# Joining the q and k products of two attentions into one token-major product of 512 columns

## Chip, cores and metric

One core of a Trainium2 chip runs the whole kernel. The metric is device time in microseconds (us). The kernel before takes 2263.23 us, the median of three runs (2261.22 to 2263.38).

## What is computed

One block of a hybrid model, for 512 tokens of width 2048: a normalization, one wide input projection, four mixers side by side, a gate and an output projection with the residual. Each mixer has 1024 columns. Cut to what matters here:

```python
h = rms_norm(x, norm_g)
p = h @ w_in                                  # 2048 -> all inputs of the mixers and the gate z
p_rwkv, p_fox, p_gdn, p_diff, z = split(p)
y = concatenate([
    rwkv7_time_mix(p_rwkv, ...),              # recurrence over tokens, 16 heads of 64
    forgetting_attention(p_fox, ...),         # q, k normalized per head of 64; softmax with forget bias
    gated_deltanet(p_gdn, ...),               # chunked delta rule, 8 heads of 128
    differential_attention(p_diff, ...),      # q, k normalized per head of 64; two softmax maps, subtracted
])
x = x + (y * silu(z)) @ w_out
```

Both attentions normalize q and k over heads of 64 columns before the scores.

## The kernel before

**Products.** All large products run on TensorE in a split form: an operand is cast to a short format (`hh`, `wh`), the remainder is kept beside it (`hl`, `wl`), and three matrix multiplies (hh·wh, hl·wh, hh·wl) stand for one. The normalized input lies in `hh` and `hl`, 16 tiles of 128 rows by 512 tokens. Weights come in tiles of 1024 columns by 128 partitions: SP issues the load into `wr` (three buffers), ScalarE casts it into `wh` (line 313, two buffers), VectorE subtracts to get `wl` (line 314, two buffers).

**Two forms of product.** `gemm_fm` is feature-major: 128 weight columns are the stationary operand, 512 tokens move, one accumulator bank, 48 multiplies. `gemm_tm` is token-major: 128 tokens are stationary, 256 weight columns move (128 each of two column blocks, `ca` and `cb`), 192 multiplies of 256 columns for all 512 tokens, in two accumulator banks of two token tiles each. It runs over four weight parts; with `late` (used for `fqk` alone) the order is part 0 and part 1 of the first bank, then both parts of the second. There are two banks of the kind `acc`; the products take them in turn.

**The loop.** `main()` is one stream over eight groups `j`. A group's products are, in order: r, k, v of the recurrence; v, k, q of the delta rule (`gv`, `gk`, `gq`); `fqk` (q and k of the forgetting attention); `vv` (the values of both attentions; for group 0 made ahead, and two gate products stand in its place); `dqk` (q and k of the differential attention). Everything else (recurrence chain, delta chain, triangular inverses, the attentions) is written as generators, the threads, that issue a few small instructions and yield the time until they want to go on.

**The planner.** The order of TensorE's instructions is written out by the program: a clock `pe[0]` adds up modelled TensorE time, and a thread whose time has come puts its instructions between two steps of the stream. A yielded time is stretched by `SLACK = 1.25`. The stream may also yield a condition, such as `("gdn_chain", j - 1)` after the `gk` product; until it holds, threads alone go on. PSUM banks have planned times: `bank(tag, name, hold)` takes one, `release(name, wait)` says when it comes free, `free(tag)` waits for it. The delta chain holds its bank `cg` for one chunk of 128 tokens, four chunks in a row. The other engines' orders are found by a scheduler, by the bands of priority that `band()` sets: chains first, then weight loads and splits, read-outs of products, the rest. Each engine, and each queue for loads and stores, serves its instructions in that order.

**q and k of an attention.** `qk_evac` reads each bank out on ScalarE (a square and two copies) and sums the squares on VectorE; `qk_heads` makes the inverse roots (`rsqrt`, three Newton steps on VectorE), scales, transposes on TensorE and splits q and k. `fox` uses the first pair of `qa` tiles, `diff` waits for `fox` and uses the next. The masks `ones`, `tri` and `sgt` lie in the pool of constants `cp`.

Of the kernel before, what the change touches and what calls it, by code (L numbers as in the profile page):

```python
# [10 lines left out]
F32 = mybir.dt.float32  # L11
# [3 lines left out]
AF = mybir.ActivationFunctionType  # L15
# [39 lines left out]
def hybrid_kernel(ctx: ExitStack, tc: tile.TileContext, ins, out, steps=tuple(range(NJ)), ydbg=None, tail=True):  # L55
# [124 lines left out]
    def mm_tm(accs, t, part, wh, wl, ks=range(4), paired=False):  # L180
        o = accs[t // 2][:, (t % 2) * 256:(t % 2) * 256 + 256]
        ts_ = slice(t * P, (t + 1) * P)
        if paired:
            for k4 in ks:
                k = part * 4 + k4
                sl = slice(k4 * 256, (k4 + 1) * 256)
                MM(o, hh[:, k, ts_], wh[:, sl], start=(k == 0 and t % 2 == 0), stop=False)
                MM(o, hh[:, k, ts_], wl[:, sl], start=False, stop=False)
                MM(o, hl[:, k, ts_], wh[:, sl], start=False, stop=(k == KT - 1 and t % 2 == 1))
            return  # L190
# [36 lines left out]
    for t in range(NT):  # L227
# [23 lines left out]
        for part in range(4):  # L251
            wr, wh, wl = w0[part]
            if t == 0:
# [7 lines left out]
    ones = cp.tile([P, P], F32, name="ones")  # L261
    nc.gpsimd.memset(ones, 1.0)
    tri = cp.tile([P, P], F32, name="tri")
    nc.gpsimd.affine_select(out=tri, in_=ones, pattern=[[1, P]], compare_op=ALU.is_ge,
                            fill=0.0, base=0, channel_multiplier=-1)
    sgt = cp.tile([P, P], F32, name="sgt")
    nc.gpsimd.affine_select(out=sgt, in_=ones, pattern=[[-1, P]], compare_op=ALU.is_gt,
                            fill=0.0, base=0, channel_multiplier=1)
# [5 lines left out]
    mask2 = cp.tile([P, P], F32, name="mask2")  # L274
    for half in range(2):
        rows = slice(half * C, (half + 1) * C)
        nc.gpsimd.affine_select(out=mask2[rows, 0:C], in_=ones[rows, 0:C], pattern=[[1, C]],
                                compare_op=ALU.is_gt, fill=0.0, base=0, channel_multiplier=-1)
        nc.gpsimd.affine_select(out=mask2[rows, C:], in_=ones[rows, 0:C], pattern=[[1, C]],
                                compare_op=ALU.is_ge, fill=0.0, base=0, channel_multiplier=-1)  # L280
# [61 lines left out]
    def gemm_tm(ca, cb, name, evac, need, late=False):  # L342

        accs, ws = None, {}
        order = [(part, b) for part in range(4) for b in range(2)]
        if late:
            order[0:4] = [(0, 0), (1, 0), (0, 1), (1, 1)]
        for part, b in order:
            if part not in ws:
                band(PRIO_W)  # L350
                wr = wtile()
                load_tm(wr, part, ca, cb)
                ws[part] = wsplit(wr)
            for t in (2 * b, 2 * b + 1):
                for k4 in (0, 2):
                    band(PRIO_GEMM)
                    if accs is None:
                        accs = [pacc(f"acc_{name}_{i}") for i in range(2)]
                    mm_tm(accs, t, part, *ws[part], (k4, k4 + 1), name.startswith("fqk"))
                    yield  # L360
            if part == 3:
                yield need
                band(PRIO_EVAC)
                evac(b, accs[b])

# [103 lines left out]
    def gates(fab0):  # L469
        fold = mp.tile([C, 32], F32, name="fold", tag="at", bufs=4)  # L470
# [412 lines left out]
    def gdn_chain(j, st, XG):  # L883
# [3 lines left out]
        for c in range(NT):  # L887
# [21 lines left out]
            MM(ps[:, 3 * P:4 * P], GA[:, c, 1, :], Y, start=True, stop=True)  # L909
            if c < NT - 1:  # L910
                band(PRIO_CHAIN)
# [4 lines left out]
                band(PRIO_MIX)  # L916
            if c:
                ACT(ot[:, c, :], ps[:, P:2 * P], AF.Copy, scale=eg[:, 0, c, j:j + 1])
# [3 lines left out]
            release(f"pG{j}_{c}", 5.0)  # L922
# [138 lines left out]
    def qk_evac(j, kind):  # L1061
        tiles = []

        def evac(b, acc):
            if b == 0:
                tiles.extend(mp.tile([P, NT, P], F32, name=f"{s}a{kind}{j}", tag="qa", bufs=2) for s in "qk")
                tiles.append(mp.tile([P, 16], F32, name=f"ss{kind}{j}", tag="ss", bufs=2))
            qa, ka, ss = tiles
            av = acc.rearrange("p (t s f) -> p t s f", t=2, s=2)
            sq = mp.tile([P, T], F32, name=f"sq{kind}{j}_{b}", tag="tmp", bufs=2)  # L1070
            ACT(sq, acc, AF.Square)
            for s, dst in enumerate((qa, ka)):
                nc.scalar.copy(dst[:, 2 * b:2 * b + 2, :], av[:, :, s])
            nc.vector.tensor_reduce(ss[:, 8 * b:8 * b + 8], sq.rearrange("p (g f) -> p g f", f=C),
                                    axis=AX.X, op=ALU.add)

        return tiles, evac

    def qk_heads(j, ev, kind):
        qa, ka, ss = ev  # L1080
        gi = 0 if kind == "fox" else 2
        TS(ss, ss, 1.0 / C, 1e-6, op0=ALU.mult, op1=ALU.add)
        rs = rsqrt(mp, ss, 16, "qk", f"{kind}{j}")
        yield 3.0
        rv = rs.rearrange("p (t s h) -> p t s h", t=NT, s=2)
        for s, dst in enumerate((qa, ka)):
            dv = dst.rearrange("p t (h f) -> p t h f", f=C)
            TT(dv, dv, rv[:, :, s].unsqueeze(3).to_broadcast([P, NT, 2, C]), op=ALU.mult)
# [3 lines left out]
        for s, src in enumerate((qa, ka)):  # L1092
# [94 lines left out]
    def diff(j, ev, V):  # L1187
        yield from until("fox", j)
# [93 lines left out]
    def main():  # L1282
# [15 lines left out]
        for j in steps:  # L1298
# [37 lines left out]
            spawn(2.0, fox(j, fev, values, nb))  # L1336
# [154 lines left out]
```

## Time and profile before

| what | value |
|---|---|
| median of three runs | 2263.23 us |
| the profiled execution's own time | 2262.35 us |
| its span, first to last instruction | 2260.5 us |
| TensorE busy (PE) | 2221.2 us, 98% |
| weight loads into TensorE (PEld) | 1906.3 us, 84% |
| VectorE (DVE) | 1370.0 us, 61% |
| ScalarE (ACT) | 795.5 us, 35% |
| GpSimd (POOL) | 228.3 us, 10% |
| mean granted TensorE clock | 0.994 of full speed |
| moved by DMA | 225.81 MB, mean 100 GB/s |

A busy TensorE is not one at its peak: matrix multiplies overlap, so the distance between two starts tells more than the length of one. In the timeline a row gives start, duration, engine, line, operation, out<-in, shapes and count; a bracket at the end is the idle time before it and what ended it. The group around 1083 us, used below, is group 5 of the loop.

### The profile page before, as it was taken

The numbers are of one execution on the slowest core, as the hardware profiler recorded it, in microseconds if no ns is written. First come the engines' busy times: TensorE is split into PE (matmuls) and PEld (weight loads), VectorE is DVE, ScalarE is ACT, GpSimd is POOL, SyncE is SP. The second block draws the span as 40 slices with busy tenths as digits, with TensorE's granted clock in tenths as the row PEclk, the third lists the DMA queues.
The fourth block names the chain that finished last, engine by engine and source line by source line (L and its number), as shares of the span: only waits on it lengthen the run. The fifth ranks groups of instructions, "written<-read, shape, count | busy, mean of one in ns | idle before, by whom it ended". The sixth has DMA issues, their size and how long they took to land.

```text
span 2260.5 us, 37244 instructions
## 1 busy us (share of the span) xinstructions
PE 2221.2 (98%) x14604; PEld 1906.3 (84%) x14604; DVE 1370.0 (61%) x3601; ACT 795.5 (35%) x1456; POOL 228.3 (10%) x474
## 2 busy tenths in 40 slices
PE   7999999999999999999999999999999999999999
PEld 6789789879978977987997897798888888888887
DVE  6368487677856858767785785876553334322222
ACT  4233443343343344334334334433332233321121
POOL 2200121102102112110210201211000000100000
PEclk9999999999999999999999999999999999999999
DMA  5433323323322332332332233233346444655443
GB/s 167 104 87 95 96 70 94 96 61 89 97 72 72 89 97 70 94 97 63 87 102 65 74 87 96 67 99 101 99 139 178 120 123 121 164 135 117 113 124 75
DMA packets 320850, 225.81 MB, mean 100 GB/s; under 512 B 16911, under 2 KB 284370, under 8 KB 320162
## 3 DMA queue, kind: packets, MB, share of 16 engines
q1 hardware_dynamic: 298722, 187.05, 31.3%
q0 software_dynamic: 8128, 14.84, 3.0%
q10 hardware_dynamic: 13824, 21.54, 2.9%
q8 instruction: 115, 1.88, 0.4%
q14 instruction: 61, 0.50, 0.1%
HBM read 203.40 MB, written 19.97 MB: 99 GB/s over the span
## 4 chain that ended last, share of the span: by engine, by line
PE 95%; DVE 2%; DMA 1%; ACT 1%; issue 1%; POOL 1%; ACTq 0%; SPq 0%; DVEq 0%; POOLq 0%
PE acc_z L70 16%; PE acc_o L70 15%; PE acc_fqk L70 8%; PE acc_dqk L70 8%; PE acc_vv L70 8%; PE acc_v L70 4%; PE acc_k L70 4%; PE acc_r L70 4%; PE acc_gk L70 4%; PE acc_gv L70 4%; PE acc_gq L70 3%; PE pC L70 3%; PE pm L70 1%; PE pG L70 1%; PE pSf L70 1%; PE po L70 1%
## 5 line engine op out<-in xcount | busy, mean ns | idle before, releaser
L314 DVE TENSOR_TENSOR wl<-wr,wh 128x1024 fp32r<-128x1024 f32 x318 | 388.7, 1223 | 535.8 <-ACT wh L313 529.8
L313 ACT CAST wh<-wr 128x1024 fp32r<-128x1024 f32 x318 | 333.8, 1050 | 770.3 <-PE acc_o L70 232.1
L70 PE MATMUL acc_z<-hh,wh 128*128 128x512 f32 x512 | 204.5, 399 | 0.0
L70 PE MATMUL acc_z<-hh,wl 128*128 128x512 f32 x512 | 199.8, 390 | 0.0
L70 PE MATMUL acc_z<-hl,wh 128*128 128x512 f32 x512 | 199.6, 390 | 0.0
L70 PE MATMUL acc_o<-wh,gl 128*128 128x512 f32 x512 | 183.6, 389 | 0.0
L70 PE MATMUL acc_o<-wl,gh 128*128 128x512 f32 x512 | 177.4, 389 | 0.0
L70 PE MATMUL acc_o<-wh,gh 128*128 128x512 f32 x512 | 176.2, 389 | 0.1
L70 PE MATMUL acc_fqk<-wh,hh 128*128 128x256 f32 x512 | 151.1, 295 | 0.0
L70 PE MATMUL acc_fqk<-wl,hh 128*128 128x256 f32 x512 | 145.2, 284 | 0.0
L70 PE MATMUL acc_fqk<-wh,hl 128*128 128x256 f32 x512 | 145.1, 283 | 0.0
L70 PE MATMUL acc_dqk<-wh,hh 128*128 128x256 f32 x512 | 138.3, 292 | 0.0
L70 PE MATMUL acc_dqk<-wh,hl 128*128 128x256 f32 x512 | 133.6, 283 | 0.0
L970 DVE TENSOR_TENSOR bP<-bX,bA 112x2 f32<-112x2 f32 (+30 forms) x248 | 122.0, 492 | 5.6 <-POOL bA L958 1.1
L70 PE MATMUL acc_vv<-wh,hh 128*128 128x256 f32 x448 | 120.7, 291 | 0.0
L70 PE MATMUL acc_vv<-wh,hl 128*128 128x256 f32 x448 | 116.9, 282 | 0.0
L70 PEld LDWEIGHTS acc_z<-hh,wl 128*128 128x128 f32 x512 | 96.1, 188 | 20.7
L70 PEld LDWEIGHTS acc_o<-wh,gh 128*128 128x128 f32 x512 | 96.0, 188 | 20.4 <-ACT wh L313 0.5
L70 PEld LDWEIGHTS acc_z<-hh,wh 128*128 128x128 f32 x512 | 96.2, 188 | 19.9 <-issue 0.7
L70 PEld LDWEIGHTS acc_o<-wl,gh 128*128 128x128 f32 x512 | 96.1, 188 | 20.0
L70 PEld LDWEIGHTS acc_o<-wh,gl 128*128 128x128 f32 x512 | 96.1, 188 | 20.0
L70 PEld LDWEIGHTS acc_z<-hl,wh 128*128 128x128 f32 x512 | 96.3, 188 | 18.3
(514 smaller groups left out, 5210.6 us busy)
## 6 DMA issues: line engine op xcount, KB each, us to landing
wr<-in_w_in SPq DMA_DIRECT2D x162, 512.0 KB
wr<-in_w_in SPq DMA_DIRECT2D x184, 256.0 KB
wr<-in_w_out SPq DMA_DIRECT2D x64, 512.0 KB
zy<-ydr ACTq DMA_DIRECT2D x30, 256.0 KB
nb<-cdr SPq DMA_DIRECT2D x8, 512.0 KB
xo<-in_x ACTq DMA_DIRECT2D x16, 256.0 KB
gr<-gdr POOLq DMA_DIRECT2D x16, 256.0 KB, 4.7
out<-xo ACTq DMA_DIRECT2D x16, 256.0 KB
```

Of the source, the lines that this page charges most:

```text
L70: return nc.tensor.matmul(o, a, b, **kw)
L313: nc.scalar.copy(wh[:, 0:n], wr[:, 0:n])
L314: TT(wl[:, 0:n], wr[:, 0:n], wh[:, 0:n].bitcast(F32), op=ALU.subtract)
L970: TT(pv_, X[:, 0:n, 0:w], A[:, 0:w, t].unsqueeze(1).to_broadcast([112, n, w]), op=ALU.mult)
```

## The change

The two q,k products of a group become one, `gemm_qk`: 128 tokens are stationary and 512 weight columns move (128 each of the q and k columns of both attentions). A token tile then fills a bank, so the tokens go in two halves of two tiles, and each half loads and splits all eight weight tiles of two k-steps anew (four loads of 128 columns per tile). `qk_evac` now reads out one token tile at a time: the forgetting attention's q and k go to `qa` tiles as before, those of the differential attention to a tile `qkl` (two buffers) and from there by a POOL DMA to DRAM; `diff` fetches them by two POOL DMAs when the forgetting attention's q and k are done. One `rsqrt` of 32 columns serves both attentions. `dqk` goes from the loop, `late` and `paired` go from `gemm_tm`. In the delta chain a ScalarE read of the bank moves ahead, the last subtraction gets the chain's priority, and the bank is released after 3.2 instead of 5.0. The masks `ones`, `tri`, `sgt` move into a tile of `gates` that shares the place of `nb`.

```diff
-    def gemm_tm(ca, cb, name, evac, need, late=False):
-
+    def gemm_tm(ca, cb, name, evac, need):
         accs, ws = None, {}
-        order = [(part, b) for part in range(4) for b in range(2)]
-        if late:
-            order[0:4] = [(0, 0), (1, 0), (0, 1), (1, 1)]
-        for part, b in order:
+        for part, b in [(part, b) for part in range(4) for b in range(2)]:
...
+    def gemm_qk(j, evac, need):
+
+        cols = [c + j * P for c in (FOX0, FOX0 + G, DIFF0, DIFF0 + G)]
+        for half in range(2):
+            accs, ws = None, {}
+
+            order = [(i, b) for i in range(6) for b in range(2)] + [(6, 0), (7, 0), (6, 1), (7, 1)]
+            for i, b in order:
+                if i not in ws:
+                    band(PRIO_W)
+                    wr = wtile()
+                    wv = wr.rearrange("p (k n) -> p k n", n=T)
+                    for s, c in enumerate(cols):
+                        nc.sync.dma_start(wv[:, :, s * P:(s + 1) * P], w_in_v[:, 2 * i:2 * i + 2, c:c + P])
+                    ws[i] = wsplit(wr)
+                wh, wl = ws[i]
+                t = 2 * half + b
+                ts_ = slice(t * P, (t + 1) * P)
+                for k2 in range(2):
+                    band(PRIO_GEMM)
+                    if accs is None:
+                        accs = [pacc(f"acc_qk{j}_{half}{b_}") for b_ in range(2)]
+                    k = 2 * i + k2
+                    sl = slice(k2 * T, (k2 + 1) * T)
+                    MM(accs[b], hh[:, k, ts_], wh[:, sl], start=(k == 0), stop=False)
+                    MM(accs[b], hl[:, k, ts_], wh[:, sl], start=False, stop=False)
+                    MM(accs[b], hh[:, k, ts_], wl[:, sl], start=False, stop=(k == KT - 1))
+                    yield
+                if i == 7:
+                    if t == 0:
+                        yield need
+                    band(PRIO_EVAC)
+                    evac(t, accs[b])
...
                 STT(rs, ps[:, 0:P], eg_neg[:, c, j:j + 1], vn[:, c, :], op0=ALU.mult, op1=ALU.add)
                 band(PRIO_MIX)
+                ACT(ot[:, c, :], ps[:, P:2 * P], AF.Copy, scale=eg[:, 0, c, j:j + 1])
...
             if c:
-                ACT(ot[:, c, :], ps[:, P:2 * P], AF.Copy, scale=eg[:, 0, c, j:j + 1])
                 TT(ot[:, c, :], ot[:, c, :], ps[:, 3 * P:4 * P], op=ALU.subtract)
             else:
                 TS(ot[:, c, :], ps[:, 3 * P:4 * P], -1.0, None, op0=ALU.mult)
-            release(f"pG{j}_{c}", 5.0)
+            band(PRIO_MIX)
+            release(f"pG{j}_{c}", 3.2)
...
+    def qk_evac(j):
+
+        st = {"wait": dr.tile([NT, P, 256], F32, name=f"qkd{j}", tag="qkd", bufs=2)}
+
+        def evac(t, acc):
+            if t == 0:
+                st["fox"] = [mp.tile([P, NT, P], F32, name=f"{s}afox{j}", tag="qa", bufs=2) for s in "qk"]
+                st["ss"] = mp.tile([P, NT, 8], F32, name=f"ss{j}", tag="ss", bufs=2)
+            sq = mp.tile([P, T], F32, name=f"sq{j}_{t}", tag="tmp", bufs=2)
             ACT(sq, acc, AF.Square)
+            for s, dst in enumerate(st["fox"]):
+                nc.scalar.copy(dst[:, t, :], acc[:, s * P:(s + 1) * P])
+            later = mp.tile([P, 256], F32, name=f"qkl{j}_{t}", tag="qkl", bufs=2)
+            nc.scalar.copy(later, acc[:, 256:512])
+            nc.gpsimd.dma_start(st["wait"][t], later)
+            nc.vector.tensor_reduce(st["ss"][:, t, :], sq.rearrange("p (g f) -> p g f", f=C), axis=AX.X, op=ALU.add)
+
+        return st, evac
...
     def diff(j, ev, V):
+        yield from until("fox_qk", j)
+        ev["diff"] = [mp.tile([P, NT, P], F32, name=f"{s}adiff{j}", tag="qa", bufs=2) for s in "qk"]
+        for s, dst in enumerate(ev["diff"]):
+            nc.gpsimd.dma_start(dst, ev["wait"][:, :, s * P:(s + 1) * P].rearrange("t p f -> p t f"))
         yield from until("fox", j)
...
-            fev, evac = qk_evac(j, "fox")
-            yield from gemm_tm(FOX0 + j * P, FOX0 + G + j * P, f"fqk{j}", evac, ("diff_qk", j - 1), True)
+            ev, evac = qk_evac(j)
+            yield from gemm_qk(j, evac, ("diff_qk", j - 1))
...
-            dev, evac = qk_evac(j, "diff")
-            yield from gemm_tm(DIFF0 + j * P, DIFF0 + G + j * P, f"dqk{j}", evac, ("fox_qk", j))
-            spawn(2.0, diff(j, dev, V[:, :, P:256]))
+            spawn(2.0, diff(j, ev, V[:, :, P:256]))
```

## Rows read from the trace of the kernel before

**Rows 1.** The page: busy time per engine, and the chain of waits by engine

```profile
PE 2221.2 (98%) x14604; PEld 1906.3 (84%) x14604; DVE 1370.0 (61%) x3601; ACT 795.5 (35%) x1456; POOL 228.3 (10%) x474
...
PE 95%; DVE 2%; DMA 1%; ACT 1%; issue 1%; POOL 1%; ACTq 0%; SPq 0%; DVEq 0%; POOLq 0%
```

**Rows 2.** TensorE's waits: who for whom, us in total, times, longest

```profile
PE pC L70 <- ACT yt L719: 4.3, 5, 1.5
...
PE pG L70 <- DVE dso L1218: 0.4, 1, 0.4
```

**Rows 3.** Stretches: length, busy PE, PEld, DVE, ACT, POOL, clock, DMA share, GB/s

```profile
1060.70:1070.70 10.00, 8.03 (x79) 6.47 (x78) 8.49 (x27) 4.67 (x10) 1.79 (x4) 1.00 0.23 59
...
1139.60:1167.80 28.20, 28.20 (x243) 26.46 (x242) 27.30 (x67) 11.69 (x27) 0.00 (x0) 1.00 0.28 76
1167.80:1213.50 45.70, 45.70 (x348) 36.29 (x347) 21.72 (x59) 17.34 (x40) 6.30 (x12) 1.00 0.35 96
...
1083.80:1138.00 54.20, 54.20 (x468) 53.43 (x467) 40.01 (x124) 19.81 (x34) 7.33 (x16) 1.00 0.36 99
```

**Rows 4.** Chain of waits in time: start, us, engine, what, multiplies

```profile
695.38 3.84 PE acc_gq L70 x9
...
1074.66 2.82 PE acc_gq L70 x12
...
1112.32 2.88 PE acc_vv L70 x24
...
1697.37 210.17 PE acc_z L70 x927
```

**Rows 5.** Timeline, TensorE, ScalarE, VectorE: delta q product's end and read-out, groups 5, 3

```profile
1083.59 0.40 PE L70 MATMUL acc_gq<-hh,wl 128*128 128x512 f32 x1
1083.82 0.28 PE L70 MATMUL acc_fqk<-wh,hh 128*128 128x256 f32 x1
...
1084.53 0.60 PE L74 MATMUL pgk<-ident,gc_k 128*128 128x128 f32 x4
...
1085.14 0.68 ACT L791 ACTIVATE gc_q<-acc_gq,vec 128x512 f32<-128x512 f32 x1
...
1088.78 0.73 DVE L793 SCALAR_TENSOR_TENSOR gc_q<-acc_gq,vec,gc_q 128x509 f32<-128x509 f32 x1
...
709.88 0.39 PE L70 MATMUL acc_gq<-hh,wl 128*128 128x512 f32 x1
...
714.52 0.75 DVE L793 SCALAR_TENSOR_TENSOR gc_q<-acc_gq,vec,gc_q 128x509 f32<-128x509 f32 x1
```

**Rows 6.** Timeline, TensorE and ScalarE: end of fqk and its read-out

```profile
1111.60 0.28 PE L70 MATMUL acc_fqk<-wh,hl 128*128 128x256 f32 x1
...
1111.96 1.05 ACT L313 CAST wh<-wr 128x1024 fp32r<-128x1024 f32 x1 [1.79 <-issue]
...
1113.66 0.38 ACT L1073 COPY kafox<-acc_fqk 128x256 f32<-128x256 f32 x1
```

**Rows 7.** Timeline, TensorE, ScalarE, VectorE: fqk's first tile done, its buffer split anew

```profile
1094.14 0.28 PE L70 MATMUL acc_fqk<-wh,hl 128*128 128x256 f32 x1
...
1094.92 1.03 ACT L313 CAST wh<-wr 128x1024 fp32r<-128x1024 f32 x1
...
1095.98 1.23 DVE L314 TENSOR_TENSOR wl<-wr,wh 128x1024 fp32r<-128x1024 f32 x1 [0.24 <-ACT wh L313]
```

**Rows 8.** VectorE's groups, 1083.8 to 1139.6: busy us, mean ns, idle before

```profile
L1074 DVE TENSOR_REDUCE ssfox<-sqfox 128x8 f32<-128x512 f32 x2 | 1.4, 677 | 0.0
...
L160 DVE TENSOR_TENSOR rsq_qkfox<-rsy_qkfox 128x16 f32<-128x16 f32 x3 | 0.5, 172 | 0.1
```

**Rows 9.** Half a microsecond while one weight tile lands: clock, DMA share, GB/s

```profile
1109.50:1110.00 0.50, 1.00 1.14 343
```

**Rows 10.** Timeline, TensorE: first multiplies after two holes while the delta chain ends

```profile
690.12 0.45 PE L70 MATMUL pC<-rs,ET 128*66 128x64 f32 x4 [1.51 <-ACT yt L719]
...
1065.17 0.66 PE L74 MATMUL pB<-ident,BK 128*128 128x128 f32 x4 [0.68 <-ACT prd L1142]
```

More of the change, by code (lines that the diff above doesn't have):

```diff
@@ L178, in load_tm, with mm_tm @@
         nc.sync.dma_start(wv[:, :, P:256], w_in_v[:, ks, cb:cb + P])
-    def mm_tm(accs, t, part, wh, wl, ks=range(4), paired=False):
+    def mm_tm(accs, t, part, wh, wl, ks=range(4)):
         o = accs[t // 2][:, (t % 2) * 256:(t % 2) * 256 + 256]
         ts_ = slice(t * P, (t + 1) * P)
[L183 to L190, printed above, removed]
         for k4 in ks:
@@ L260, in hybrid_kernel @@
     band(PRIO_W)
[L261 to L268, printed above, removed]
     zb = mp.tile([P, P], BF16, name="zb")
@@ L274, in hybrid_kernel @@
     mask2 = cp.tile([P, P], F32, name="mask2")
+    nc.gpsimd.memset(mask2, 1.0)
     for half in range(2):
         rows = slice(half * C, (half + 1) * C)
-        nc.gpsimd.affine_select(out=mask2[rows, 0:C], in_=ones[rows, 0:C], pattern=[[1, C]],
+        nc.gpsimd.affine_select(out=mask2[rows, 0:C], in_=mask2[rows, 0:C], pattern=[[1, C]],
                                 compare_op=ALU.is_gt, fill=0.0, base=0, channel_multiplier=-1)
-        nc.gpsimd.affine_select(out=mask2[rows, C:], in_=ones[rows, 0:C], pattern=[[1, C]],
+        nc.gpsimd.affine_select(out=mask2[rows, C:], in_=mask2[rows, C:], pattern=[[1, C]],
                                 compare_op=ALU.is_ge, fill=0.0, base=0, channel_multiplier=-1)
@@ L358, in gemm_tm @@
                         accs = [pacc(f"acc_{name}_{i}") for i in range(2)]
-                    mm_tm(accs, t, part, *ws[part], (k4, k4 + 1), name.startswith("fqk"))
+                    mm_tm(accs, t, part, *ws[part], (k4, k4 + 1))
                     yield
@@ L469, in gates @@
     def gates(fab0):
+        sums = mp.tile([P, 3, P], F32, name="sums", tag="nb", bufs=1)
+        tri, sgt, ones = (sums[:, i] for i in range(3))
+        nc.gpsimd.memset(sums, 1.0)
+        nc.gpsimd.affine_select(out=tri, in_=tri, pattern=[[1, P]], compare_op=ALU.is_ge,
+                                fill=0.0, base=0, channel_multiplier=-1)
+        nc.gpsimd.affine_select(out=sgt, in_=sgt, pattern=[[-1, P]], compare_op=ALU.is_gt,
+                                fill=0.0, base=0, channel_multiplier=1)
         fold = mp.tile([C, 32], F32, name="fold", tag="at", bufs=4)
@@ L909, in gdn_chain @@
             MM(ps[:, 3 * P:4 * P], GA[:, c, 1, :], Y, start=True, stop=True)
+            band(PRIO_CHAIN)
             if c < NT - 1:
-                band(PRIO_CHAIN)
                 if c:
@@ L915, in gdn_chain @@
                     nc.vector.tensor_copy(S, ps[:, 0:P])
-                band(PRIO_MIX)
             if c:
-                ACT(ot[:, c, :], ps[:, P:2 * P], AF.Copy, scale=eg[:, 0, c, j:j + 1])
                 TT(ot[:, c, :], ot[:, c, :], ps[:, 3 * P:4 * P], op=ALU.subtract)
@@ L1058, in inverses @@
         return XG
[L1061 to L1070, printed above, removed]
-            ACT(sq, acc, AF.Square)
[L1072 to L1077, printed above, removed]
@@ L1079, in qk_heads @@
-    def qk_heads(j, ev, kind):
-        qa, ka, ss = ev
+    def qk_evac(j):
[5 more added lines that the diff above has]
+            sq = mp.tile([P, T], F32, name=f"sq{j}_{t}", tag="tmp", bufs=2)
+            ACT(sq, acc, AF.Square)
+            for s, dst in enumerate(st["fox"]):
[5 more added lines that the diff above has]
+        return st, evac
@@ L1081, in qk_heads @@
+    def qk_heads(j, st, kind):
+        if kind == "fox":
+            ss = st["ss"].rearrange("p t g -> p (t g)")
+            TS(ss, ss, 1.0 / C, 1e-6, op0=ALU.mult, op1=ALU.add)
+            st["rs"] = rsqrt(mp, ss, 32, "qk", j).rearrange("p (t a s h) -> p t a s h", a=2, s=2, h=2)
         gi = 0 if kind == "fox" else 2
-        TS(ss, ss, 1.0 / C, 1e-6, op0=ALU.mult, op1=ALU.add)
-        rs = rsqrt(mp, ss, 16, "qk", f"{kind}{j}")
         yield 3.0
-        rv = rs.rearrange("p (t s h) -> p t s h", t=NT, s=2)
@@ L1086, in qk_heads @@
-        for s, dst in enumerate((qa, ka)):
+        for s, dst in enumerate(st[kind]):
             dv = dst.rearrange("p t (h f) -> p t h f", f=C)
-            TT(dv, dv, rv[:, :, s].unsqueeze(3).to_broadcast([P, NT, 2, C]), op=ALU.mult)
+            TT(dv, dv, st["rs"][:, :, gi // 2, s].unsqueeze(3).to_broadcast([P, NT, 2, C]), op=ALU.mult)
         yield 1.2
         parts = []
-        for s, src in enumerate((qa, ka)):
+        for s, src in enumerate(st[kind]):
             big, small = [mp.tile([P, T], F32R, name=f"{'QK'[s]}{n}{kind}{j}", tag=f"{'QK'[s]}{n}", bufs=1)
@@ L1332, in main @@
             nc.sync.dma_start(nb, cdr[2 * j:2 * j + 2].unsqueeze(0).to_broadcast([P, 2, T]))
-            fev, evac = qk_evac(j, "fox")
-            yield from gemm_tm(FOX0 + j * P, FOX0 + G + j * P, f"fqk{j}", evac, ("diff_qk", j - 1), True)
+            ev, evac = qk_evac(j)
+            yield from gemm_qk(j, evac, ("diff_qk", j - 1))
             values = []
-            spawn(2.0, fox(j, fev, values, nb))
+            spawn(2.0, fox(j, ev, values, nb))
             if j == 0:
```

## The prediction

> **What bounds the kernel now.** I read the page first: TensorE is busy 98% of the span, and the chain of work that ended last runs through it for 95% [rows 1]. Then I asked what TensorE waits for. The list of its waits is short: the nine rows that belong to the loop over the eight groups (pC, pdo, pgk, pB, pG) run from the first to the last row shown and sum to 18.5 us [rows 2]. So a change pays only if it takes TensorE time away, and it costs whatever makes TensorE stand still. The other engines have room on average, but VectorE has little in places: 40.01 us of 54.20 after the delta q product, 27.30 of 28.20 in the dqk product, 21.72 of 45.70 in the three products after it [rows 3]. The profiled execution took 2262.35 us (span 2260.5 and 1.85 around it), 0.9 under the median of 2263.23; the sum below is made against the former.
>
> **Term 1, wider products.** Per group, 384 matrix multiplies of 256 columns (fqk and dqk) become 192 of 512. The chain shows what one costs when they stand back to back: 24 of 256 in 2.88 us, 120.0 ns each; 927 of 512 in 210.17 us, 226.7 ns each [rows 4]. A pair costs 240.0, its replacement 226.7: 13.3 ns saved, times 192 x 8 = 1536, is 20.4 us. The other bound is the short run of 512 columns inside the loop, 12 in 2.82 us or 235 ns [rows 4], which leaves 5 ns a pair, 8 us. I take -20, the nearer row being the long run: the new product is as dense.
> The Trainium skill, page "TensorE: Matmul & The Clock Gate", section "Back-to-back issue gap", prices a warm multiply at N/2.4 + 2.5 ns. That is 109.2 for 256 columns and 215.8 for 512, a saving of 2.5 ns a pair, or 4 us in all, an estimate from that page; both of this trace's rows lie above it by about 11 ns [rows 4], so the fixed part is larger here. With the page's figure the sum below would come out 16 us later.
>
> **Term 2, the head of the new product.** It writes two accumulator banks; the second was the delta q product's, and its first multiply must wait until that product is read out. In the group shown the last delta q multiply starts at 1083.59; ScalarE reads the bank from 1085.14, the last of VectorE's three passes ends at 1088.78 + 0.73 = 1089.51, which is 5.92 us later [rows 5]. Another group gives 714.52 + 0.75 - 709.88 = 5.39 [rows 5]. Before, this costs nothing: the order called late puts 48 multiplies of 120 ns, 5.8 us, ahead of the second bank. The new order puts six of 512 ahead: 0.23 until they start, 6 x 0.227 = 1.36, and four transposes that the planner slips in, at 1084.53 [rows 5], 0.35 until the next multiply: 1.94 us in all. TensorE is served in order, so everything behind that multiply (the chains' small products included) waits too. Upper value 5.92 - 1.94 = 4.0. Lower: if no weight split (1.23, term 4) comes between the passes, 2.7. I take 3.4 x 8 = +27, range 20 to 32.
>
> **Term 3, the middle.** The second half needs the same two banks again. The order at the end (6 and 7 of the first bank, then of the second) gives the first bank 12 x 0.227 = 2.7 us of cover, the second only the 0.23 + 1.36 = 1.59 of the next half's first six. In the fqk product the last multiply starts at 1111.60, ScalarE first does a cast and has read the bank out at 1113.66 + 0.38 = 1114.04, 2.44 us after [rows 6]; the new read-out has one copy more, so about 2.6. That is 1.0 us of standing still, +8 in all. Below it is 0, where a small product or a missing cast (1.05) covers it. The value product after it has 24 multiplies of 2.88 us on its first bank, enough.
>
> **Term 4, feeding.** A split weight tile now lasts 12 x 0.227 = 2.72 us instead of 48 x 0.12 = 5.8, and each is split twice, once per token half: 8 tiles more per group, 64 in all, 1.05 us of ScalarE and 1.23 of VectorE each. Does a split fit? Before has a place with the same lead: in fqk's early order the first tile's last multiply starts at 1094.14, the cast into its buffer at 1094.92, and the remainder is ready at 1095.98 + 1.23 = 1097.21, 3.07 us after [rows 7]. The new product asks for the remainder at the tile's third multiply: 0.23 + 2.72 + 0.45 = 3.4. So it just fits, with 0.3 to spare, if both engines come as promptly. VectorE had 40.01 of the 54.20 us that the new product will about cover [rows 3]; out goes the fox normalization (four passes like the 0.75 of [rows 5], twelve short ones like the 0.17 of [rows 8]: 5), in come 8 splits (10), two more sums of the read-out (0.68 each [rows 8]: 1.4) and the differential attention's end, which moves there and which I put at 4: 50 of some 57, the stop of term 2 included. That is tight, not over. SP issues four loads a tile for two, and one tile's data moved at 343 GB/s [rows 9] where 512 KB per 2.72 us needs 193. Both ends: 0, and 0.6 us per tile, 77 us, if each split comes late by one VectorE pass (0.75 [rows 5]) less part of that slack. I take 1 us a group, +8.
>
> **Term 5, the delta bank.** At the end of each gk product the stream waits for the delta chain of the group before; in the window 1060.70 to 1070.70 TensorE is busy 8.03 of 10.00 us [rows 3], on chain steps with holes like 0.68 us [rows 10]. Releasing the bank after 3.2 instead of 5.0 moves each chunk by 1.8 x 1.25 = 2.25 us of the planner's clock, three chunks by 6.75, so most of a 10 us wait goes. What is it worth? At most the 18.5 us of [rows 2] and the granted clock: after idle stretches such as the 1.51 us at 690.12 [rows 10], nine multiplies ran at 3.84 / 9 = 427 ns [rows 4], the 1.2 GHz level, 1.8 us lost. Bounds 0 and -21; the chain's true latency stays and only holes shrink, so -10.
>
> **Term 6, the clock again.** The stops of term 2 are longer than the hole above; where one drops the clock it costs the same 1.8 us. Bounds 0 and 8 x 1.8 = 14; +3.
>
> **Hidden.** The second rsqrt (12 short VectorE instructions a group) falls away, off TensorE's path. The DRAM round trip of the second attention has more than a whole value product to land; POOL carries its six DMAs a group, and if POOL stands at a longer wait, two buffers hold the first two and ScalarE stops only at the third. The fox scores start one product later, since V comes later; they move from the stretch with 27.30 of 28.20 to that with 21.72 of 45.70 [rows 3], and the stream asks for fox only after six more products. The mask tiles' move costs nothing.
>
> **Sum.** -20 + 27 + 8 + 8 - 10 + 3 = +16: 2278.4, or 2279 against the median. What is late next is the second bank.
>
> **Rivals.** *The wait at the head is short, and the bank hold pays.* If small products of the attention, which now end later, fall into the head, 1.5 us a group stays: 12. With 0 and 2 for terms 3 and 4, -18 for term 5 and -20 for term 1 the sum is -24, 2239; between this and 2258 it is faster. For it: the 18.5 us are real and term 1 is arithmetic on rows. Against: in the group shown one set of transposes only stands in the first 1.4 us. Chance 0.36. *Feeding binds.* One mechanism: VectorE, serving in order, comes to the remainder late by more than the 0.3 us of slack, in most of the 128 tiles. At 0.6 us each with term 2 at 20 (stops overlap), it is -20 + 20 + 77 - 10 = +67, about 2330. For it: 50 of 57 us; against: splits go ahead of all but the chains, and [rows 7] held. It decides from a VectorE share of about 95%. Chance 0.12. *A wash*, gains and stops within 0.2% (4.5 us, about what a measurement of this kernel can tell from no change): 0.10. The forecast with its own range of 2268 to 2305: 0.42.
>
> **Range and chances.** 8 in 10: from 2243, which leaves out the best part of the first rival, to 2322, which leaves out most of the second. Faster by over 0.2% 0.36, within 0.10, slower 0.54 (0.42 + 0.12).
>
> **What would show it.** In the trace after: 512-column multiplies of the qk product 0.227 us apart and 1536 of them (term 1); TensorE idle at the second bank's first multiply, ended by VectorE's delta q pass (term 2) and, in the middle, by ScalarE's read-out (term 3), 3.4 and 1 us each; little idle ended by the weight remainder (term 4); gq following gk within a few us (term 5). I am wrong if TensorE does not stop at that bank, or if the stops before the delta chain were worth more than the 10 us.

## The result, and the profile after

The changed kernel takes 2335.01 us (median of 4 runs, 2333.74 to 2337.27), the kernel before beside it 2263.31: ratio 1.032, 95% interval 1.0307 to 1.0332. That is 72 us slower; forecast was 16 slower, range 2243 to 2322. The direction was right and the size was not.

The page after, TensorE's line and the chain of waits, as [rows 1]:

```profile
PE 2237.1 (96%) x13068; PEld 1826.1 (78%) x13068; DVE 1427.6 (61%) x3561; ACT 862.8 (37%) x1552; POOL 255.3 (11%) x523
...
PE 80%; DVE 12%; DMA 3%; ACT 2%; issue 2%; SPq 1%; POOL 1%; DVEq 0%; ACTq 0%; POOLq 0%
```

There are 1536 multiplies fewer, as forecast. TensorE's idle time, span less busy, was 2260.5 - 2221.2 = 39.3 and is 2333.2 - 2237.1 = 96.1: 56.8 of the 72 is standing still. Busy time has grown by 15.9, though the multiplies need less: the mean granted clock is 0.987, before 0.994. If each mean is made of the two levels, 1.2 and 2.4 GHz, 61 us ran at the lower one against 27 before, and half of the difference, 17 us, is lost: an estimate from the two means. VectorE has gone from 2% of the chain to 12%.

What TensorE waits for after (who for whom, us in total, times, longest), the answer to [rows 2]:

```profile
PE pC L70 <- ACT yt L742: 19.3, 13, 3.7
PE acc_qk L70 <- DVE wl L299: 15.6, 28, 1.6
PE acc_qk L70 <- DVE rsy_gk L156: 15.4, 6, 2.6
PE ptfox L74 <- DVE qafox L1112: 11.0, 7, 2.4
...
PE acc_vv L70 <- DVE wl L299: 3.4, 7, 0.5
PE acc_qk L70 <- DVE rsq_gk L161: 3.3, 1, 3.3
PE acc_qk L70 <- DVE gssk L830: 3.2, 1, 3.2
```

The 15.4, 3.3 and 3.2 are the second bank at the head; 15.6 and 3.4 the weight remainder; 11.0 the transposes of the forgetting attention's q and k, a stop that was not forecast; 19.3 the recurrence chain, 4.3 before. ScalarE's read-out in the middle does not appear.

Stretches after, columns as in [rows 3]: the qk product, and the time between the gk and the gq product:

```profile
932.80:995.30 62.50, 56.59 (x300) 44.63 (x299) 49.20 (x151) 28.61 (x48) 8.40 (x18) 1.00 0.57 152
1103.10:1116.00 12.90, 10.62 (x83) 8.06 (x82) 11.47 (x37) 4.43 (x11) 1.79 (x4) 0.84 0.19 47
```

VectorE works 49.2 of 62.5 us in the qk product (50 of some 57 were forecast). The last stretch answers to the 10.00 us of [rows 3]: it has grown, and the clock in it has fallen to 0.84.

Timeline after, TensorE, VectorE and ScalarE: the end of the gk product, the head of the qk product, and the forgetting attention's transposes:

```profile
1102.94 0.39 PE L70 MATMUL acc_gk<-hh,wl 128*128 128x512 f32 x1
...
1109.62 1.64 DVE L669 SCALAR_TENSOR_TENSOR ET<-pA,NV,mask 128x128 f32<-128x128 f32 x6
1111.17 0.27 DVE L740 TENSOR_TENSOR rs<-rs,pC 64x128 f32<-64x128 f32 x1
1111.47 0.26 ACT L742 COPY yt<-pC 64x128 f32<-64x128 f32 x1 [2.13 <-DVE rs L740]
1111.79 0.71 PE L70 MATMUL pC<-rs,ET 128*66 128x64 f32 x4 [2.06 <-ACT yt L742]
...
1116.06 0.77 PE L70 MATMUL acc_gq<-hh,wh 128*128 128x512 f32 x1
...
1117.06 0.63 PE L70 MATMUL acc_gq<-hh,wl 128*128 128x512 f32 x1
1117.48 0.63 PE L70 MATMUL acc_gq<-hh,wh 128*128 128x512 f32 x1
...
1131.08 0.40 PE L70 MATMUL acc_gq<-hh,wl 128*128 128x512 f32 x1
...
1132.36 1.22 DVE L299 TENSOR_TENSOR wl<-wr,wh 128x1024 fp32r<-128x1024 f32 x1 [1.87 <-ACT wh L298]
1132.44 1.06 PE L70 MATMUL pd<-V,prd 128*128 128x128 f32 x8
1134.31 0.40 PE L70 MATMUL acc_qk<-wl,hh 128*128 128x512 f32 x1
1136.39 0.73 DVE L816 SCALAR_TENSOR_TENSOR gc_q<-acc_gq,vec,gc_q 128x509 f32<-128x509 f32 x1
1137.27 0.47 PE L70 MATMUL acc_qk<-wh,hh 128*128 128x512 f32 x1 [2.56 <-DVE rsy_gk L156]
1137.58 0.39 PE L70 MATMUL acc_qk<-wh,hl 128*128 128x512 f32 x1
1137.81 0.39 PE L70 MATMUL acc_qk<-wl,hh 128*128 128x512 f32 x1
...
1202.77 0.67 DVE L993 TENSOR_TENSOR bP<-bX,bA 112x288 f32<-112x288 f32 x1
1203.36 0.18 DVE L162 SCALAR_TENSOR_TENSOR rsy_qk<-rsq_qk,rsy_qk 128x32 f32<-128x32 f32 x1
1203.47 0.45 DVE L994 TENSOR_REDUCE bX<-bP 112x12 f32<-112x288 f32 x1
1203.84 0.68 DVE L1112 TENSOR_TENSOR qafox<-qafox,rsy_qk 128x512 f32<-128x512 f32 x1
1204.67 0.63 PE L74 MATMUL ptfox<-ident,qafox 128*128 128x128 f32 x4 [1.46 <-DVE qafox L1112]
```

Three places. First, between the last gk and the first gq multiply, the recurrence's `rs` stands in VectorE's order behind six `ET`; TensorE stops for 2.06 us, and then multiplies of 512 columns start 0.42 apart, the lower level, as in [rows 4]. Second, the head as forecast: 6.0 us from the last delta q multiply to the end of VectorE's third pass (1137.12). The row names `rsy_gk` because the trace puts the wait down to what VectorE finished next. Third, the forgetting attention's inverse roots run between the steps `bP`, `bX` of the triangular solve, which take turns on VectorE.

### The profile page after: what moved, and what is told of

It reads as the page before. It is cut to its first block, busy times and chain, and to the rows that moved or that the text cites. A ratio compares the mean times of both kernels' runs of the same rounds, so it can differ in the third digit from the quotient of the medians.

```text
span 2333.2 us, 35325 instructions
## 1 busy us (share of the span) xinstructions
PE 2237.1 (96%) x13068; PEld 1826.1 (78%) x13068; DVE 1427.6 (61%) x3561; ACT 862.8 (37%) x1552; POOL 255.3 (11%) x523
## 4 chain that ended last, share of the span: by engine, by line
PE 80%; DVE 12%; DMA 3%; ACT 2%; issue 2%; SPq 1%; POOL 1%; DVEq 0%; ACTq 0%; POOLq 0%
PE acc_o L70 15%; PE acc_z L70 15%; PE acc_qk L70 9%; PE acc_vv L70 5%; PE acc_v L70 4%; PE acc_k L70 4%; DVE wl L299 4%; PE acc_r L70 4%; PE acc_gk L70 4%; PE acc_gq L70 3%; PE acc_gv L70 3%; PE pC L70 3%; DMA wr<-in_w_in 2%; DVE bP L993 1%; PE pm L70 1%
## 5 line engine op out<-in xcount | busy, mean ns | idle before, releaser
L299 DVE TENSOR_TENSOR wl<-wr,wh 128x1024 fp32r<-128x1024 f32 x382 | 466.9, 1223 | 525.3 <-ACT wh L298 512.3
L298 ACT CAST wh<-wr 128x1024 fp32r<-128x1024 f32 x382 | 401.3, 1051 | 733.3 <-PE acc_o L70 237.7
L70 PE MATMUL acc_qk<-wh,hh 128*128 128x512 f32 x512 | 212.2, 415 | 21.9 <-DVE rsy_gk L156 15.4
L70 PE MATMUL acc_qk<-wl,hh 128*128 128x512 f32 x512 | 205.4, 401 | 16.2 <-DVE wl L299 15.6
L70 PE MATMUL acc_qk<-wh,hl 128*128 128x512 f32 x512 | 201.3, 393 | 0.0
L70 PEld LDWEIGHTS acc_qk<-wl,hh 128*128 128x128 f32 x512 | 96.8, 189 | 51.1 <-DVE wl L299 30.4
L70 PEld LDWEIGHTS acc_qk<-wh,hh 128*128 128x128 f32 x512 | 96.8, 189 | 43.8 <-ACT yt L742 17.8
L70 PEld LDWEIGHTS acc_o<-wl,gh 128*128 128x128 f32 x512 | 96.1, 188 | 20.0
L70 PEld LDWEIGHTS acc_o<-wh,gl 128*128 128x128 f32 x512 | 96.1, 188 | 19.9
L70 PEld LDWEIGHTS acc_o<-wh,gh 128*128 128x128 f32 x512 | 96.1, 188 | 20.0
```

The source lines that it names most:

```text
L70: return nc.tensor.matmul(o, a, b, **kw)
L298: nc.scalar.copy(wh[:, 0:n], wr[:, 0:n])
L299: TT(wl[:, 0:n], wr[:, 0:n], wh[:, 0:n].bitcast(F32), op=ALU.subtract)
```

## The experiments

Each run is compared with the kernel before, measured beside it (medians of 2262.5 to 2263.3). "Changed" is the changed kernel. The runs with fewer splits multiply some weight tiles in the place of others, so their attention q and k are not the block's; they tell only what the splits cost.

**Feeding.** Changed, with no second set of splits: the second half multiplies the first half's last tile.

```diff
+        ws = {}
         for half in range(2):
-            accs, ws = None, {}
+            accs, ws = None, ({} if half == 0 else {i: ws[7] for i in range(8)})
```

> The changed kernel, with the second token half multiplying the last weight tile of the first half throughout: no loads, casts or remainders for that half (64 weight tiles less; this part of the product is not the reference's). Theory FEED (the double feeding costs more than the stops that TensorE shows at the remainder: it also pushes other VectorE work back): 2335 falls by 30 to 45 us, to 2290 to 2305. Rival STOPS ONLY (feeding costs the waits for the remainder, some 18 us, and no more): about 2317. Rival SHIFT (the cost is that the attentions' work now lies in the wait for the delta chain): above 2325.

2342.55 us (ratio 1.0353, 1.0338 to 1.0369), 7.5 more than changed. No wait on `wl` is left, but:

```profile
PE ptfox L74 <- DVE qafox L1113: 36.5, 8, 6.1
PE pC L70 <- ACT yt L743: 19.6, 14, 3.7
```

TensorE comes to the transposes sooner and waits there, 36.5 us for 11.0. Feeding as the one cost falls; a stop that is taken away can come back at the next place.

**The delta bank.** Changed, with the bank's part undone (release after 5.0, old place of the ScalarE read and old bands):

> The changed kernel with its delta bank part undone (5.0, the old place of the read, the old priorities). If the shorter hold gained nothing in the changed kernel because another chain sets the order's pace: 2335 within 6 us. If the hold is what makes the wait for the delta chain worse (holes of 2 us and the lower clock in every group): 10 to 25 us faster, 2310 to 2325. If it did what was forecast: about 2345.

2365.73 us (1.0457, 1.0441 to 1.0473): 31 more than changed, above all three theories. The head's stops are now 34.4:

```profile
PE acc_qk L70 <- DVE rsq_gk L161: 34.4, 8, 5.1
```

The same part alone in the kernel before (the place of the read and the bands as in the change):

```diff
...
-            release(f"pG{j}_{c}", 5.0)
...
+            release(f"pG{j}_{c}", 3.2)
```

> The kernel before with the delta bank part alone. Forecast of the prediction's term 5: -10, so about 2253. Theory OTHER PACE (the recurrence chain sets the pace, the hold is not on the path): 2263 within 4 us. Theory that it brings holes: 2270 to 2285.

2257.45 us (0.9976, 0.9967 to 0.9986): -5.6, in term 5's bounds, below its 10.

**Order.** The kernel before with `dqk` ahead of `vv`:

> The kernel before with the dqk product moved ahead of the value product, nothing else: the forgetting attention's scores start one product later, as in the changed kernel, with no double feeding and no wider product. Theory SHIFT: slower by 20 to 35 us (2283 to 2298), with the lower clock in the wait for the delta chain in most groups. Theory FEED: within 8 us of 2263.

2273.04 us (1.0042, 1.0027 to 1.0057): +10 with no wider multiply and no second splits, between what the two theories gave.

**The head.** Changed, delta q read out by one ScalarE copy, the passes from there:

```diff
+        if s == "q":
+            raw = mp.tile([P, T], F32, name=f"gr_{s}{j}", tag="tmp", bufs=2)
+            nc.scalar.copy(raw, acc)
+            acc = raw
```

> The changed kernel, with the delta q product read out by one ScalarE copy to SBUF, from which the convolution then reads: the second bank comes free after that copy (some 2 us after the last multiply) instead of after three VectorE passes (5.9). The stops at the head, 22 us of the changed kernel's trace, should go. Theory SUM (the stops add up): 2335 falls to 2310 to 2317. Theory TIED (what is saved ahead of the forgetting attention's transposes is lost at them, as in the run without second splits): 2328 to 2340, with the wait for the scaled q above 20 us.

2306.75 us (1.0192, 1.0177 to 1.0208): -28. The 21.9 us of stops at the head are gone; the 11.0 at the transposes are as they were.

**The transposes.** Changed, those of the forgetting attention planned later: 9.0 for 3.0, which with the planner's stretching is 7.5 us; then the same with no second set of splits:

```diff
-        yield 3.0
+        yield 9.0 if kind == "fox" else 3.0
```

> The changed kernel, with the forgetting attention's transposes planned 7.5 us later (9.0 for 3.0 before the scaling), so that TensorE does not come to them before VectorE is done. Theory COLLISION (its inverse roots now run between the steps of the triangular solve, and TensorE stops at the transposes, 11 us): 2335 falls by 8 to 20 us, the wait for the scaled q is under 3 us. Rival: the fox scores move too and hit the wait for the delta chain harder: no change or slower, 2330 to 2345.

> Both: the second half multiplies the first half's last tile throughout (that part is not the reference's), and the transposes are planned later. Theory COLLISION, with feeding at 2 to 3 us a group behind it: 2343 falls by 25 to 45 us to 2298 to 2318, and against the run that only plans later by 15 to 25. Rival (feeding costs nothing of its own): within 8 us of the run that only plans later.

2327.68 us (1.0296, 1.0264 to 1.0328), -7, which is not clear of the runs' own spread (2322.3 to 2338.4; changed 2333.7 to 2337.3); and 2307.46 (1.0197, 1.0181 to 1.0212), 20 below that. Without the stops at the transposes, the second splits do cost.

**The recurrence bank.** The kernel before with the delta bank's part and the recurrence bank released sooner:

```diff
-            release(f"pC{j}_{c}", 3.0)
+            release(f"pC{j}_{c}", 1.5)
```

> The kernel before with the delta bank part and the recurrence chain's bank released after 1.5 instead of 3.0. Theory OTHER PACE (the recurrence chain sets the pace of the written order, the delta bank alone is half of it): the wait for the delta chain after each gk product goes, 2263 falls by 8 to 20 us, below the 2257 of the delta bank alone. Rival (TensorE's own work binds, the waits are filled anyway): 2254 to 2260. Rival (chain steps come too early and TensorE stops at them): above 2263.

2241.85 us (0.9907, 0.9892 to 0.9922): 21 faster than before, the best of all runs. The second edit alone in the kernel before:

> The kernel before with the recurrence bank released after 1.5 alone, the delta bank as it was. Both holds together gave -21, the delta bank alone -6. Additive: -15, 2248. Theory that the two chains are in series and the slower one sets the wait: between -3 and -10, since the delta chain's 5.0 then binds. Either way it says what share of the 21 the change could have had from its own part.

2256.39 us (0.9972, 0.9961 to 0.9982): -6.4. The two give 5.6 and 6.4 singly and 21 together, as they would if the two chains were in series and the one that stays set the wait. The same edit alone in changed:

> The changed kernel with one number moved: the recurrence bank is released after 1.5 instead of 3.0 (the release that, together with the delta bank's, brought the kernel before to 2241.9). Theory CHAIN (about half of the 72 us is the wait at the end of each group for the delta chain, holes plus the multiplies at 1.2 GHz behind them): 2295 to 2315, the waits on yt shrink from 19 us to under 8, the 427 ns rows at the start of the gq product go. Rival VECTORE (the chain's steps are late because VectorE, serving in order, comes late to each, so a release moves nothing): 2328 to 2338, waits on yt as before. Rival PLAN (the steps are brought forward into the stretch where VectorE is full and collide there): above 2338.

2333.53 us (1.0313, 1.0287 to 1.0339), nothing, where the theory of the chain had 2295 to 2315. Its waits:

```profile
PE acc_qk L70 <- DVE rsy_gk L162: 27.1, 6, 4.5
PE ptfox L74 <- DVE qafox L1112: 25.2, 8, 3.3
...
PE acc_qk L70 <- DVE wl L299: 4.9, 10, 0.8
PE acc_qk L70 <- DVE rsq_gk L160: 4.8, 1, 4.8
...
PE acc_qk L70 <- DVE rsq_gk L161: 3.3, 1, 3.3
```

The chain's 19.3 us are gone, as the theory had it, and `wl` lost 10.7; the time was not won, since the head went from 21.9 to 27.1 + 4.8 + 3.3 = 35.2 and the transposes from 11.0 to 25.2, which together is 27.5 of those 30.

**Three mends together**: head copy, transposes at 9.0, recurrence bank 1.5; and the same with no second set of splits.

> The changed kernel with the three mends found so far together: delta q read out by one ScalarE copy (alone -28), fox transposes planned later (alone -7), recurrence bank released after 1.5. Theory CHAIN, with the parts additive: 2335 - 28 - 7 - 25 to 35 = 2265 to 2275, about the kernel before or a little above. Rival SHIFT (what is left is that the longer product ahead of the value product pushes all attention work later, whatever its waits): 2285 to 2300, with small waits spread over many rows. Under 2250 would say that the wider products pay as forecast once the waits are gone.

> The kernel with the three mends, and the second token half multiplied with the first half's last weight tile throughout: no loads, casts or remainders for the second half (its q and k are then not the reference's). Theory FEEDING (a second set of splits costs 20 us with the fox transposes out of the way): 18 to 25 us below the kernel with the three mends, 2245 or so, the waits on the weight remainder gone. Rival (feeding only mattered through the waits mended here): within 6 us of it.

2299.44 us (1.0161, 1.0146 to 1.0176) and 2268.03 (1.0022, 1.0013 to 1.0032). The first is what -28 and -7 give, as if the bank again added nothing (no run has the other two alone); its theory had 2265 to 2275. In it TensorE waits for:

```profile
PE pC L70 <- ACT yt L742: 20.2, 15, 2.5
...
PE pgv L74 <- ACT yg L969: 8.1, 4, 2.0
```

**What was left.** Two runs with fewer splits (every second tile taken for its neighbour; the second run also makes none for the second half), and two that move a product: the second attention's ahead of the values in the best kernel, and the values ahead of the wide product in the one with the three mends.

```diff
+                if i % 2:
+                    ws[i] = ws[i - 1]
                 if i not in ws:
```

> The kernel with the three mends; every split weight tile is multiplied for two tiles' worth (tile 1 uses tile 0's split, 3 uses 2's, in both token halves), so that a split is asked for every 5.4 us throughout, eight in a group as in the kernel before; the q and k are then not the reference's. The run with eight splits crowded into the first half stands at 2268. Theory CROWDING (splits every 2.7 us take VectorE from the small steps of the delta output and the recurrence, which stop TensorE): 2240 to 2255, the waits on yg and yt in the qk product go. Theory PLACE (the long product in that place sets it, not the splits): 2262 to 2275.

> As the one before, and the second token half splits nothing at all: four splits a group, half of what the kernel before makes, so VectorE has some 5 us a group and ScalarE 4 us less than there. Theory CROWDING: 2230 to 2245. Theory PLACE: 2258 to 2272. If even this stays above 2242, the wider multiplies pay nothing in this order of work, whatever feeds them.

> The kernel before with both banks released sooner (2242), and the second attention's q and k product moved ahead of the value product: the order of the changed kernel with narrow multiplies and the old feeding. Moving it cost 10 in the kernel before. Theory PLACE: +15 to +40, 2257 to 2280. Theory CROWDING: 0 to +12, at most 2254.

> The kernel with the three mends (2299), the value product moved ahead of the wide product, so that what VectorE and ScalarE have to do after the delta q product is met by 25 us of narrow multiplies with a split every 5.8 us. Theory CROWDING: 2260 to 2285, since VectorE is less full where the small steps stand. Theory PLACE: within 10 of 2299 or above, since fox then starts later still (its scores some 27 us after where they stood), and the delta wait at the end of the group grows.

2270.09 us (1.003, 1.0017 to 1.0043) and 2265.83 (1.0012, 1.0003 to 1.0021): neither spreading nor halving the splits helps beyond 2268, so crowding falls. The third: 2241.94 (0.9907, 0.9892 to 0.9922): the order costs nothing once both banks come free sooner, so place falls too. The fourth: 2360.69 (1.0433, 1.0418 to 1.0449), worse by 61. The attentions start later still, but the wait for the delta chain, which was to grow, is nearly gone (the time from gk to gq is 6.1 us over seven ends of groups, 22.9 before the move); TensorE waits for `wl` (29.9 us in the wide product) and for the second attention (21.4). The clue is in the trace with four splits, TensorE, stops of two groups that follow each other:

```profile
685.81 0.45 PE L70 MATMUL pC<-rs,ET 128*66 128x64 f32 x4 [2.06 <-ACT yt L745]
699.52 0.49 PE L70 MATMUL pd<-V,prd 128*128 128x128 f32 x2 [3.34 <-ACT prd L1173]
...
876.43 0.45 PE L70 MATMUL pC<-rs,ET 128*66 128x64 f32 x4 [0.36 <-ACT yt L745]
893.64 0.49 PE L70 MATMUL pd<-V,prd 128*128 128x128 f32 x2 [0.81 <-ACT prd L1173]
901.74 0.45 PE L70 MATMUL pC<-rs,ET 128*66 128x64 f32 x4 [1.92 <-ACT yt L745]
```

Short and long groups take turns (183.7 and 192.4 us the next two), and the stops are about their end, where the second attention (`pd`) and the recurrence still run. So the last two runs plan the transposes at 6.0 instead of 9.0, 3.75 us sooner, in the kernel with splits spread and in the one with the three mends, which computes everything:

> The kernel with the three mends and eight splits a group spread evenly (each split tile multiplied for two tiles' worth, so q and k are not the reference's; 2270), fox transposes planned later by 6 instead of 9. Theory TAIL (the second attention, pushed too far back, runs into the end of the group and the recurrence is waited for there in every second group): all groups near 183.5 us, waits on yt under 8 us in all, 2225 to 2245, so that the wide multiplies pay 0 to 18 against the narrow kernel with the same order and releases (2242). Rival (the alternation comes from VectorE and stays): 2262 to 2275.

> The same mend in the kernel that computes everything (2299 with 9): the changed kernel with delta q read out by a ScalarE copy, recurrence bank released after 1.5, fox transposes planned later by 6. Theory TAIL, with the second set of splits still to be paid (20 to 31): 2250 to 2275. Rival: 2292 to 2305. The gap to the run beside it is then the whole price of feeding the wide product twice as often.

2260.04 us (0.9987, 0.9977 to 0.9997) and 2258.34 (0.998, 0.997 to 0.9989). The second has fallen by 41 for one number, and is 4 us faster than the kernel before; below it is the mended kernel. The first has fallen by 10 only, where its theory had 25 or more: with half the splits it is no faster than the second, since waits at the transposes (18.0 us, 7 times) take the place of those on `wl`. The waits of the second:

```profile
PE acc_qk L70 <- DVE wl L299: 12.9, 16, 1.3
...
PE acc_vv L70 <- DVE wl L299: 3.8, 7, 0.6
PE pC L70 <- ACT yt L742: 3.6, 1, 3.6
...
PE acc_qk L70 <- ACT qkl L1101: 1.6, 6, 0.3
```

## Why the prediction was wrong

**Term 1, wider products: right in price.** Chain of waits, start, us, multiplies; first the narrow kernel with both banks and the second attention's product moved:

```profile
162.04 10.79 PE acc_fqk L70 x90
```

and the mended kernel:

```profile
1118.67 8.01 PE acc_qk L70 x35
```

That is 119.9 ns for 256 columns and 228.9 for 512: 10.9 a pair, 17 us in 1536; forecast 20. By the formula of the Trainium skill ("TensorE: Matmul & The Clock Gate", "Back-to-back issue gap"), which stands there for an isolated multiply without the cost of a weight load, it would be 4, an estimate; the measured rows decide.

**Term 2, the head: right.** 21.9 us of stops, 28 with all that hangs on them (the run with the head copy); forecast 27.

**Term 3, the middle: too high.** No stop in changed, 1.6 us in all in the mended kernel, forecast 8. In the group shown ScalarE leaves the second bank at 1167.85 (2.9 us after its last multiply starts; 2.6 were forecast) and the bank's next multiply starts at 1167.90: four transposes (0.35) and a stop on `wl` (0.61) stood ahead of it. The cover that the term named as its lower end was there.

**Term 4, feeding: too low.** 15.6 + 3.4 = 19 us of waits on `wl`, forecast 8; 16.7 in the mended kernel. VectorE's load was near the forecast, but the argument took an average. The waits sit at the same few places of each group. Two follow from the order at a half's end, (6, 0), (7, 0), (6, 1), (7, 1), whose lead the term did not look at: tile 7 is asked for after six multiplies of tile 6, not twelve (0.88 us in the group shown), and the first tile of the second half gets tile 6's buffer only eight multiplies before its own remainder is due (0.61). What it costs is not additive: to take the second set of splits away wins 20 us in one kernel and 31 in another, and loses 7 in a third; in the last kernel, half the splits, spread evenly, win nothing (2260 against 2258).

**The step that failed: terms 5 and 6, and "hidden".** It was said that the bank makes the wait for the delta chain at the end of gk shrink, that the clock costs 3, and that a later start of the forgetting attention costs nothing. The bank's part does pay (5.6, and 31 in the new kernel), and alone in the kernel before it does shorten the time from the last gk to the first gq multiply, from 42.8 us over seven ends of groups to 25.3; the 10.00 us of [rows 3] were the longest of the seven. But in the changed kernel that time grew, to 79.2. The table gives, in us after the last delta q multiply, one group for each kernel (that multiply starts between 704 and 907 us), then the sum over the seven ends and the kernel's time:

| kernel | forgetting scores start | delta chain | last gk | first gq | gk to gq, seven ends | time |
|---|---|---|---|---|---|---|
| before | 58 | 126 to 172 | 167 | 172 | 42.8 | 2263 |
| changed | 89 | 141 to 182 | 169 | 182 | 79.2 | 2335 |
| three mends, 9.0 | 96 | 136 to 179 | 175 | 180 | 22.9 | 2299 |
| three mends, 6.0 (mended) | 85 | 126 to 169 | 171 | 171 | 2.0 | 2258 |
| best (both banks) | 55 | 118 to 164 | 172 | 172 | 1.6 | 2242 |
| best, second attention's product moved | 83 | 124 to 167 | 169 | 169 | 1.8 | 2242 |
| changed, recurrence bank 1.5 | 95 | 136 to 179 | 181 | 181 | 1.8 | 2334 |
| three mends, values first | 140 | 107 to 154 | 194 | 194 | 6.1 | 2361 |

"First gq" follows the chain's end or the last gk multiply, whichever is later. In changed the chain starts 15 us later and 13 us pass between gk and gq. What TensorE does there is sparse, its stops of 2 us are followed by the lower level, and 17 us go to the clock where 3 were forecast. Where they go can be estimated as length times (1 - granted clock) of a stretch: 19 us about the seven ends of groups (from the last gk multiply to 5 us behind the first of gq), 5 before; at the eight heads, where term 6 looked for it, 4 (12 us from the last delta q multiply), 2 before.

That the chain is late because the forgetting attention's inverse roots run into the solve, and its scores into what stands between solve and chain, is read from the timelines. The run that plans it 3.75 us earlier bears it out: of its 41 us, 21 are won between gk and gq and 16 ahead of the last gk multiply (in the third row's kernel only every second group is as shown; in the others gq follows gk by 1.2). Gk and gq in the mended kernel:

```profile
1060.49 0.40 PE L70 MATMUL acc_gk<-hh,wl 128*128 128x512 f32 x1
1060.72 0.40 PE L70 MATMUL acc_gq<-hh,wh 128*128 128x512 f32 x1
```

The run with the values first does not bear it out: its scores start latest, yet its chain ends 20 to 40 us ahead of the last gk multiply in all but the first group, and its 61 us lie elsewhere.

A chain that ends in time is also not enough. With the recurrence bank released sooner, gq follows gk at once in the changed kernel, and the time stays. Gk and gq, and the head behind them:

```profile
1104.15 0.40 PE L70 MATMUL acc_gk<-hh,wl 128*128 128x512 f32 x1
1104.38 0.40 PE L70 MATMUL acc_gq<-hh,wh 128*128 128x512 f32 x1
...
1126.64 0.77 PE L70 MATMUL acc_qk<-wh,hh 128*128 128x512 f32 x1 [4.55 <-DVE rsy_gk L162]
1127.21 0.63 PE L70 MATMUL acc_qk<-wh,hl 128*128 128x512 f32 x1
1127.64 0.63 PE L70 MATMUL acc_qk<-wl,hh 128*128 128x512 f32 x1
```

The stop at the head is now 4.55 us, the multiplies behind it start 0.57 and 0.43 apart, and the clock's loss has moved: nothing about the ends of groups, 23 us at the heads. The run with the bank's part undone says the same from the other side: 56.4 us from gk to gq in place of 79.2, and 31 us slower. So the late chain is one place where the cost shows, and no price that is saved by itself. Of the runs that compute everything with the wide product, only the one with the head copy, the recurrence bank and the planned delay of 6.0 together won it back: 2335 to 2258, product and feeding unchanged.

So the account of the 72 is, by the page, 57 more of standing still and 16 more of busy time. The stops: about 22 us at the head, 19 on `wl`, 11 at the transposes and 15 more on the recurrence make 67, less 12 of the stops of before ([rows 2]) that are gone: 55. The busy time: -17 for term 1 and 17 for the clock cancel, and the 16 that were measured are not explained by any run. As the runs trade one stop for another, none of these is what its removal alone would win.

The rival "feeding binds" came nearest in time (2330) by luck, with the wrong mechanism: 19 of its 77 us were there, at a VectorE share of 0.79 in the product where it wanted about 0.95. What stays open: which of the mends the last 41 us need (the recurrence bank was not put back in the last kernel), and why that kernel stays 16 above the best with the moved order. Its idle time is 2256.9 - 2207.4 = 49.5 against 2241.0 - 2212.7 = 28.3, so 21 of stops against 5 of busy time saved; where the other 12 of term 1's 17 went, no run took apart. No version with wide products beat 2241.85.

## What to carry to other kernels

Where TensorE's order is fixed in advance, do not price a change's stops one by one from their place. Ask when each long chain now ends against the product that waits for it, and what the other engines will be asked for at the next place once it ends in time: here one release time closed the wait for the chain, and the same time came back at the head and the transposes. An edit that wins nothing alone may be worth 40 us after the next mend, so try mends together. Wider multiplies saved what the rows said, and still paid less than two release times changed in the kernel before.

## What the runs showed of the hardware

The clock fell behind some stops and not behind others. In the changed kernel, behind a stretch of small products and a stop of 2.06 us, the next multiplies of 512 columns start 0.57, 0.43, 0.42, 0.43, 0.43 and 0.36 us apart (from 1116.06) before they come back to 0.23; a stop of 2.06 at this place is followed by such spacings in six groups of six. The longer stop of 2.56 us at the head, behind mostly dense products, was not: the next multiplies start 0.31 and 0.23 apart (from 1137.27), in six groups of six. Stops of 3.2 to 3.3 us at the head (the first two groups) and of 4.5 and more (with the recurrence bank released sooner) were followed by 0.43. In the mended kernel the loop has one stop over 1.4 us, of 3.6 us at 325 us, with six multiplies at the lower level behind it, and the mean granted clock is 0.998. And with a weight load for every multiply, 256 columns more cost 228.9 - 119.9 = 109.0 ns, so that the wider form wins 10.9 ns a pair.
